# A gate chain on 32 rows, retention tiles normalised in pairs, and three kinds of stores issued one step later

## The chip, the cores and the metric

The kernel runs on one core of a Trainium2 chip. A core has five engines that work side by side: TensorE (PE, with PEld for its weight loads), VectorE (DVE), ScalarE (ACT), GpSimd (POOL) and SyncE (SP). In this kernel SP does almost nothing but issue DMA transfers, in the order in which the program put them into its queue. The engines wait for each other by semaphores, and each carries out its own instructions strictly in order. An instruction that waits therefore also holds up whatever stands behind it on its engine.

The metric is the time of one execution on the device in microseconds (us). Before the change it is 2268.21 us, the median of three runs.

## The reference

The input is one sequence of 1024 rows by 1024 columns. Two layers of the same form follow each other. Each has eight heads of width 256: four mLSTM heads, whose gates depend on the data, and four retention heads, whose decay is fixed. Cut to what matters here:

```python
for l in range(2):
    shift, scale, gate = split(silu(c) @ w_ada[l] + b_ada[l], 3)
    h = rmsnorm(x, norm_g[l]) * (1 + scale) + shift
    mq, mk, mv, mo, mz, mi, mf, rq, rk, rv, rz = split_cols(h @ w_in[l])
    # mLSTM: four heads; mi and mf are one number per row and head
    li, lf = mi + b_igate[l], log_sigmoid(mf + b_fgate[l])
    #   b = cumsum(lf); running maximum m of (li - cumsum(lf)); weights exp(... - m)
    cell = mlstm_chunkwise(silu(conv(mq)), silu(conv(mk)), mv, li, lf)
    y_m = sigmoid(mo) * head_layernorm(cell, gn_m[l]) * silu(mz)
    # retention: four heads; o_t = sum over s <= t of gamma^(t-s) (q_t . k_s) v_s
    ret = retention_chunkwise(rotary(rq), rotary(rk), rv)
    y_r = head_layernorm(ret, gn_r[l]) * silu(rz)
    x = x + gate * (concat(y_m, y_r) @ w_out[l])
return rmsnorm(x, final_g)
```

"Gates" in what follows means the two numbers per row and head, `mi` and `mf`. From them come three running quantities over the 1024 rows of each head: the sum of the coarse part and of the fine part of log sigmoid (`bq`, `br`), and a running maximum (`mx`).

## The kernel before

**Products.** All large products are in fp32, made of three fp32r matmuls each (L177, L178, L179: high by high, high by low, low by high part). The projections use a Strassen-Winograd scheme. Two heads or column groups form a "pair", and a pair needs seven products, named a12, a11, S2, S1, S3, a22, S4, each in two parts for the values. One product of one part is a "slot". A slot of the value stage has 24 matmuls of 256 columns. Products that share a PSUM bank add up in it: a11, S2, S3 and a22 of one part all go through bank X (`px`), so the slot a22 can start only when the sum after S3 has been read out by DVE (L824).

**Steps.** After every slot the program calls `tick()`. Small generators do all side work: a generator does a piece, says `yield n`, and gets its next piece n ticks later (`launch`, L149). PE keeps the order in which the program is written. Each other engine gets an order that a planner sets from its own estimate of times, except for instructions inside `late(...)` (and calls on `Later()`, which wraps every call in it), which keep the order of the program.

**The layer.** At the start of a layer stand the gates' own products (`pgs`, in PSUM bank `pa`), then the chain on the gates, then the value stage of heads 4 and 5 (`v45`), further value, gate and query/key jobs, and the attention of one head after another (retention heads 4 to 7, then mLSTM heads 0 to 3). The order of jobs is a string per layer (`plan`).

**The gate chain (L505 to about L600).** The gates of four heads lie in 4 partitions, 1024 rows along the free axis, in two halves of 512. Bias, absolute value, Exp and Ln run on ACT (L516 to L524). Twelve ticks later some 15 DVE instructions of 4x512 follow for each half; since they are made through `V = Later()`, the trace shows them all at one line, L144. The scans of the second half start from the last column of the first. Results are gathered in a tile `T4` (in the trace `cH` and `cL`), and eight PE transposes of 128x128 (L562) turn them so that rows lie on partitions. `mx` also goes to DRAM (`mdr`, L553) and comes back as `ME` (L567).

**Normalisation (L1153 to L1190).** A retention or mLSTM head is worked through in four chunks j of 256 rows, each of two tiles of 128 rows. In the retention heads some chunks have both tiles computed in one step (j in `WHOLE`), others in two. For a tile: copy from PSUM to `n` (ACT, L1144), mean and variance (DVE, L1160, L1161), `va` (DVE, L1174), the power -1/2 (POOL, L1175), `nmu` (DVE, L1178), scale and shift (ACT, L1180). When both tiles are done, `finish` transposes them (DVE, L1188) into the single buffer `zt` and stores that to DRAM (`ndr`, L1193). `n` too is a single buffer.

**Stores.** `store` (L785 to L798) splits finished values in a high part (ACT, L789) and a low part (DVE, L792 or L794), and a tick later puts two DMA issues into SP's queue (`vdr`, L798). `z_gate` and `o_gate` do the same with gates of the output path (`gdr`, L840 and L848). All of these tiles are buffers of `acc`, of which there are 12 (`NACC`), shared by many jobs. A buffer is free again when its store has read it.

## Time and profile before

| | before |
|---|---|
| runs | 2268.85, 2267.9, 2268.21 us |
| median | 2268.21 us |
| profiled execution, own time | 2268.18 us |
| its span, first to last instruction | 2266.5 us |
| time around the span | 1.7 us |
| mean granted TensorE clock | 0.979 |
| DMA traffic | 448.31 MB, 198 GB/s |

The profiled execution lies 0.03 us below the median. PE is the engine with the largest busy share; the rest of its time consists of waits, and of stretches in which the granted clock is below 1.00, so that a matmul takes longer though PE counts as busy. Where one view gives a row such as "PE px L177 <- DVE acc L824: 12.3, 2, 7.4", PE stood still at a matmul of line 177 that writes `px`, until DVE's instruction of line 824 (which writes `acc`) was done: 12.3 us in all, 2 times, 7.4 us the longest. In rows of the timeline the first number is the start in us from the span's start, the second the duration, and in brackets stands the idle time ahead of the instruction and what ended it. An `x4` behind a row means four instructions in a run.

### The profile page before, as it was taken

What the parts mean: (1) busy time and instruction counts of PE and PEld (TensorE: products, weight loads), DVE (VectorE), ACT (ScalarE), POOL (GpSimd) and SP (SyncE); (2) the same over time, 40 slices, a digit from 0 to 9 for tenths busy, and PEclk for the clock granted to TensorE, in tenths of its full rate; (3) what the DMA queues carried; (4) which work ended last, traced back from release to release, by engine and by line L of the source; (5) the groups of instructions that cost most, each with busy time, mean ns of one, the idle gap of its engine ahead of it and who ended that gap; (6) DMA issues with size and microseconds to landing.
All of it is one profiled execution on the core that took longest, in us unless ns stands there. A gap on an engine that the chain in (4) does not pass through costs nothing.

```text
span 2266.5 us, 35156 instructions
## 1 busy us (share of the span) xinstructions
PE 2151.5 (95%) x11483; PEld 1832.0 (81%) x11483; DVE 1817.5 (80%) x3205; ACT 1159.4 (51%) x2163; POOL 964.3 (43%) x842
## 2 busy tenths in 40 slices
PE   7988999999999999999999799999999899999998
PEld 5787789878898878788778678988987888788886
DVE  6899888989979998784738989788797889977653
ACT  7634345444565656553555434543565565655442
POOL 1443244445454454424366235544544453442313
PEclk9999999999999999999999899999999999999999
DMA  8266688787686777686633767776866686686974
GB/s 285 61 176 186 188 230 249 215 235 202 185 247 175 194 203 186 175 270 210 225 107 84 214 185 210 214 198 185 245 166 192 175 238 186 173 216 203 261 245 118
DMA packets 452549, 448.31 MB, mean 198 GB/s; under 512 B 191219, under 2 KB 309755, under 8 KB 452365
## 3 DMA queue, kind: packets, MB, share of 16 engines
q1 hardware_dynamic: 432636, 410.14, 58.9%
q0 software_dynamic: 19584, 35.66, 10.4%
q8 instruction: 90, 1.47, 0.3%
q14 instruction: 95, 0.77, 0.1%
q10 hardware_dynamic: 144, 0.26, 0.0%
HBM read 322.69 MB, written 123.24 MB: 197 GB/s over the span
## 4 chain that ended last, share of the span: by engine, by line
PE 57%; DVE 22%; DMA 10%; issue 5%; POOL 2%; ACT 2%; SPq 1%; DVEq 0%; POOLq 0%; ACTq 0%
PE px L177 8%; PE px L178 8%; PE px L179 8%; PE pz L179 6%; PE pz L178 6%; PE pz L177 6%; PE pa L177 4%; PE pa L179 4%; PE pa L178 4%; DVE acc L881 3%; DVE R L408 2%; PE pa L1123 2%; DVE acc L626 2%; DMA acc<-kfr 1%; PE pa L1032 1%
## 5 line engine op out<-in xcount | busy, mean ns | idle before, releaser
L403 ACT CAST wH<-R 128x512 fp32r<-128x512 f32 x616 | 377.2, 617 | 476.6 <-PE px L178 133.0
L408 POOL TENSOR_TENSOR R<-R,wH 128x512 fp32r<-128x512 f32 x276 | 397.5, 1447 | 479.5 <-ACT wH L403 325.9
L177 PE MATMUL px<-b,wH 128*128 128x512 f32 x912 | 364.8, 400 | 8.2 <-ACT acc L767 7.4
L179 PE MATMUL px<-b,R 128*128 128x512 f32 x912 | 365.7, 401 | 0.0
L178 PE MATMUL px<-b,wH 128*128 128x512 f32 x912 | 364.8, 400 | 0.0
L408 DVE TENSOR_TENSOR R<-R,wH 128x512 fp32r<-128x512 f32 x340 | 257.2, 760 | 90.5 <-ACT wH L403 87.5
L178 PE MATMUL pz<-b,wH 128*128 128x512 f32 x704 | 280.2, 398 | 1.3 <-DVE b L1262 1.3
L179 PE MATMUL pz<-b,R 128*128 128x512 f32 x704 | 281.0, 399 | 0.0
L177 PE MATMUL pz<-b,wH 128*128 128x512 f32 x704 | 279.8, 397 | 0.2 <-ACT acc L767 0.2
L177 PEld LDWEIGHTS px<-b,wH 128*128 128x128 f32 x912 | 174.6, 191 | 48.1 <-ACT acc L767 8.9
L179 PEld LDWEIGHTS px<-b,R 128*128 128x128 f32 x912 | 174.0, 191 | 42.0 <-POOL R L408 0.8
L178 PEld LDWEIGHTS px<-b,wH 128*128 128x128 f32 x912 | 174.4, 191 | 39.3
L177 PE MATMUL px<-wH,b 128*128 128x256 f32 (+1 forms) x576 | 177.7, 309 | 27.4 <-DVE acc L824 12.3
L178 PE MATMUL px<-R,b 128*128 128x256 f32 (+1 forms) x576 | 174.9, 304 | 3.7 <-DVE R L408 3.7
L179 PE MATMUL px<-wH,b 128*128 128x256 f32 (+1 forms) x576 | 175.8, 305 | 0.0
L701 POOL DMA_DIRECT2D R<-in_w_blk_dram x104 | 92.1, 886 | 185.3 <-DMA R<-in_w_blk_dram 90.8
L178 PEld LDWEIGHTS pz<-b,wH 128*128 128x128 f32 x704 | 133.5, 190 | 32.0 <-DVE b L1262 2.2
L179 PEld LDWEIGHTS pz<-b,R 128*128 128x128 f32 x704 | 133.3, 189 | 31.5
L177 PEld LDWEIGHTS pz<-b,wH 128*128 128x128 f32 x704 | 133.8, 190 | 29.4 <-ACT acc L767 0.6
L177 PEld LDWEIGHTS px<-wH,b 128*128 128x128 f32 x576 | 115.5, 201 | 32.2 <-ACT acc L817 10.4
L179 PE MATMUL pz<-wH,b 128*128 128x256 f32 (+1 forms) x448 | 134.0, 299 | 0.4 <-DVE b L1262 0.4
L177 PE MATMUL pz<-wH,b 128*128 128x256 f32 (+1 forms) x448 | 134.0, 299 | 0.0
(357 smaller groups left out, 5346.7 us busy)
## 6 DMA issues: line engine op xcount, KB each, us to landing
R<-in_w_blk_dram SPq DMA_DIRECT2D x276, 256.0 KB
vdr<-acc SPq DMA_DIRECT2D x128, 256.0 KB
ring<-vdr SPq DMA_DIRECT2D x64, 512.0 KB
R<-in_w_out_dram SPq DMA_DIRECT2D x128, 256.0 KB
R<-in_w_blk_dram POOLq DMA_DIRECT2D x104, 256.0 KB, 4.7
R<-in_w_val_dram SPq DMA_DIRECT2D x80, 256.0 KB
gdr<-acc SPq DMA_DIRECT2D x64, 256.0 KB
acc<-in_w_ada_dram SPq DMA_DIRECT2D x64, 256.0 KB
```

Of the source, the lines that this page charges most:

```text
L177: PE.matmul(o, lt[0], rt[0], start=start, stop=False, skip_group_check=more)
L178: PE.matmul(o, lt[0], rt[1], start=False, stop=False, skip_group_check=more)
L179: PE.matmul(o, lt[1], rt[0], start=False, stop=stop, skip_group_check=more)
L403: A.copy(h, r)
L408: eng.tensor_tensor(lo, r, f(h), ALU.subtract)
L626: V.tensor_tensor(t, f(pair[0]), f(pair[1]), ALU.add)
L701: G.dma_start(raw[n], src, accum_op=ALU.add)
L881: V.scalar_tensor_tensor(acc[:, e:], pt[:, o + e - d:o + HALF - d], wcol, acc[:, e:], ALU.mult, ALU.add)
L1032: PE.matmul(pd, piece(kx[j], i, dt, tt * P, P), qd, start=dt == 0 and i == 0, stop=dt == 1 and i == 1)
L1123: PE.matmul(pi[:, 0:W], piece(qs[j], i, dt, tt * P, P), state[part][:, dt, 0:W], start=part + dt + i == 0, stop=ml and part + dt == 2)
```

## The change

It has three parts.

1. **The gate chain on 32 partitions.** The 1024 rows of the four heads are cut in 8 blocks of 128, so that 4 heads x 8 blocks give 32 partitions with 128 columns. To get there, the biased gates go to DRAM (`gtd`, two stores) and come back in the new shape (two loads). Scans then run inside a block. What one block hands to the next is made by small products on PE: a 32x32 triangular matrix times the last column of each scan (new L547, two matmuls of 32x1), a transpose of the 32 block maxima to one row (new L556), and one matmul that takes the scanned row back to a column (new L561). At the end four PE transposes of 128x32 (new L571) stand in for the eight of 128x128. The chain is stretched over more ticks: it yields 3, 3, 2, 3, 3, 3, 2, 2.
2. **Retention tiles normalised in pairs.** `normalise` is launched once for each chunk, after its second tile, with `va`, power and `nmu` on 128x2.
3. **Stores one tick later.** `yield 1` becomes `yield 2` ahead of the stores of values (L798), of gates (L840, L848) and of heads (L1193).

```diff
@@ -206,6 +206,7 @@
+    gtd = [dpool.tile([2, NH, T], F32, name=f"gtd{l}") for l in range(DEPTH)]
...
@@ -505,63 +506,70 @@
         bg = cols[l][1]
         COL = wt("COL", 8 * 16, 1)
         C4 = COL.rearrange("p (t k h) -> p t k h", t=8, k=4)
-        prev = {}
-        on4 = ones.to_broadcast([P, 512])
-        lfs, lis_, es = [], [], []
-        mxs, fbs, lif = wt("q", 1024, 2), wt("q", 1024, 2), wt("kc", 1024, 1)
+        raw = wt("kc", 1024, 1)
         for half in range(2):
-            pg = pgs[half]
...
-            V.tensor_tensor(lf[0:4], lf[0:4], lfq[0:4], ALU.subtract)
-            bq, br = e, wt("zt", 512, 1) if half else wt("n", 512, 1)
-            yield 1
-            V.tensor_tensor_scan(bq[0:4], on4[0:4], lfq[0:4], prev.get("bq", 0.0), ALU.mult, ALU.add)
-            V.tensor_tensor_scan(br[0:4], on4[0:4], lf[0:4], prev.get("br", 0.0), ALU.mult, ALU.add)
...
-            T4s.append(T4)
-            yield 1
+            for r in (0, 32):
+                A.activation(raw[r:r + 4, half * HALF:(half + 1) * HALF], pgs[half][r:r + 4, :], AF.Identity,
+                             bias=bg[r:r + 4, :])
+        for i in range(2):
+            Q.dma_start(gtd[l][i], raw[32 * i:32 * i + 4, :])
+        one, two = (wt("q", 1024, 2) for _ in range(2))
+        e, bq, br, fb, lfq, lir, tmp, small = (one[0:32, i * P:(i + 1) * P] for i in range(8))
+        u, v, mx, s, li, liq = (two[0:32, i * P:(i + 1) * P] for i in range(6))
+        lower, inc, exc, first = (small[:, i * 32:(i + 1) * 32] for i in range(4))
+        carry = two[0:32, 6 * P:6 * P + 4]
+        on = ones[0:32].to_broadcast([32, P])
+        G.memset(lower, 1.0)
+        l3 = lower.rearrange("p (h t) -> p h t", h=4)
+        G.affine_select(l3, l3, [[-8, 4], [0, 8]], ALU.is_ge, 0.0, base=0, channel_multiplier=1)
+        G.affine_select(lower, lower, [[1, 32]], ALU.is_ge, 0.0, base=-1, channel_multiplier=-1)
+        nc.vector.memset(first, 1.0)
+        nc.vector.memset(first.rearrange("p (h t) -> p h t", h=4)[:, :, 0:1], 0.0)
+        nc.vector.memset(exc, 0.0)
         yield 3
-        for half in range(2):
-            T4 = T4s[half]
-            pt = ps_a()
-            for i in range(4):
-                PE.transpose(pt[:, i * P:(i + 1) * P], T4[:, i * P:(i + 1) * P], ident)
-            V.tensor_copy(C4[:, half * 4:(half + 1) * 4],
-                          pt.rearrange("p (t k h) -> p t k h", t=4, k=4)[:, :, :, 0:4])
+        for i, t in enumerate((fb, li)):
+            Q.dma_start(t, gtd[l][i].rearrange("h (b t) -> (h b) t", t=P))
+        yield 3
+        A.activation(e, fb, AF.Abs)
+        A.activation(e, e, AF.Exp, scale=-1.0)
+        A.activation(e, e, AF.Ln, bias=ones[0:32, 0:1])
+        yield 2
+        V.scalar_tensor_tensor(fb, fb, 0.0, e, ALU.min, ALU.subtract)
+        V.tensor_scalar(lfq, fb, MAG_Q, -MAG_Q, ALU.add, ALU.add)
+        V.tensor_tensor(fb, fb, lfq, ALU.subtract)
+        V.tensor_tensor_scan(bq, on, lfq, 0.0, ALU.mult, ALU.add)
+        V.tensor_tensor_scan(br, on, fb, 0.0, ALU.mult, ALU.add)
+        V.tensor_scalar(liq, li, MAG_Q, -MAG_Q, ALU.add, ALU.add)
+        V.tensor_tensor(lir, li, liq, ALU.subtract)
+        yield 3
+        pc = ps_a()
+        for i, b in enumerate((bq, br)):
+            PE.matmul(pc[0:32, i:i + 1], lower, b[:, P - 1:P], start=True, stop=True)
+        V.tensor_copy(carry[:, 0:2], pc[0:32, 0:2])
+        for i, b in enumerate((bq, br)):
+            V.tensor_scalar(b, b, carry[:, i:i + 1], None, ALU.add)
+        V.tensor_tensor(u, liq, bq, ALU.subtract)
+        V.tensor_tensor_scan(mx, on, u, 0.0, ALU.mult, ALU.max)
+        V.tensor_tensor(v, lir, br, ALU.subtract)
+        yield 3
+        pm = ps_a()
+        PE.transpose(pm[0:1, 0:32], mx[:, P - 1:P], ident[0:32, 0:32])
+        V.tensor_tensor_scan(inc[0:1], first[0:1], pm[0:1, 0:32], 0.0, ALU.mult, ALU.max)
+        V.tensor_tensor(exc[0:1, 1:32], inc[0:1, 0:31], first[0:1, 1:32], ALU.mult)
+        yield 3
+        pb = ps_a()
+        PE.matmul(pb[0:32, 0:1], exc[0:1, :], ones[0:1, 0:1], start=True, stop=True)
+        V.tensor_copy(carry[:, 2:3], pb[0:32, 0:1])
+        V.tensor_scalar(mx, mx, carry[:, 2:3], None, ALU.max)
+        V.tensor_tensor(s, bq, mx, ALU.add)
+        V.tensor_tensor(s, s, br, ALU.add)
+        yield 2
+        Q.dma_start(mdr[l].rearrange("h (b t) -> (h b) t", t=P), mx)
...
@@ -792,7 +800,7 @@
                 V.scalar_tensor_tensor(vL, src, -1.0, f(vH), ALU.mult, ALU.subtract)
             else:
                 V.tensor_tensor(vL, src, f(vH), ALU.subtract)
-            yield 1
+            yield 2
             dst = vdr[l][heads[i]][half * 2 + part].rearrange("(i t p) c -> i p t c", i=2, p=P)
...
         if store is not None:
-            yield 1
+            yield 2
             late(Q.dma_start(store, g))
...
         V.scalar_tensor_tensor(g, th, 1.0, g, ALU.add, ALU.mult)
-        yield 1
+        yield 2
         late(Q.dma_start(store, g))
...
-            elif tts[-1] == 1:
-                launch(normalise(j, (0, 1), [nd3[:, tt, 0:HD] for tt in range(2)]), 1)
+                    A.copy(nrm[j][:, tt, :], po[:, 0:HD])
+            if tts[-1] == 1:
+                launch(normalise(j, [nrm[j][:, tt, 0:HD] for tt in range(2)]), 1)
 
         def gather(nd, po):
...
-            n, a, b = len(tts), tts[0], tts[-1] + 1
+        def normalise(j, src):
             st6 = wt("st6", 12, 2)
...
@@ -1168,25 +1171,26 @@
                 V.tensor_tensor(r, r, gt["em3"][:, h, 2 * j:2 * j + 2], ALU.max)
                 V.scalar_tensor_tensor(va, r, EPS, r, ALU.mult, ALU.mult)
                 V.tensor_tensor(va, va, mv3[:, :, 1], ALU.add)
-                G.tensor_tensor(rs, va, mhalf[:, 0:2], ALU.pow)
             else:
-                e = C_EPS + 2 * h + place(2 * j + a)
-                V.tensor_tensor(va, mv3[:, a:b, 1], kc[:, e:e + n], ALU.add)
-                G.tensor_tensor(rs, va, mhalf[:, 0:n], ALU.pow)
+                e = C_EPS + 2 * h
+                if j in WHOLE:
+                    V.tensor_tensor(va, mv3[:, :, 1], kc[:, e:e + 2], ALU.add)
+                else:
+                    V.tensor_scalar(va, mv3[:, :, 1], kc[:, e:e + 1], None, ALU.add)
+            G.tensor_tensor(rs, va, mhalf[:, 0:2], ALU.pow)
             yield 1
-            nmu = wt("nmu", 2, 2)[:, 0:n]
-            late(V.scalar_tensor_tensor(nmu, mv3[:, a:b, 0], -1.0, rs, ALU.mult, ALU.mult))
-            for i, tt in enumerate(tts):
-                late(A.activation(nrm[j][:, tt, :], src[tt], AF.Identity, scale=rs[:, i:i + 1], bias=nmu[:, i:i + 1]))
-            if tts[-1] == 1:
-                yield 1
-                yield from finish(j)
+            nmu = wt("nmu", 2, 2)
+            late(V.scalar_tensor_tensor(nmu, mv3[:, :, 0], -1.0, rs, ALU.mult, ALU.mult))
+            for tt in range(2):
+                late(A.activation(nrm[j][:, tt, :], src[tt], AF.Identity, scale=rs[:, tt:tt + 1], bias=nmu[:, tt:tt + 1]))
+            yield 1
+            yield from finish(j)
 
         def finish(j):
...
-            yield 1
+            yield 2
```

The instructions of two engines at the places that matter most. First PE in layer 0 (the value stage of heads 6 and 7), before: the eight transposes of the gate chain stand between two slots; `ident` is the identity, `cH` and `cL` are the two T4 tiles, `pz` and `px` banks of value products.

```order
843 L178 MATMUL pz_2214<-R_2098,b_1263 128x256
844 L179 MATMUL pz_2214<-wH_2096,b_1264 128x256
845 L562 MATMUL pa_2241<-ident,cH_1770 128x128 x4
846 L562 MATMUL pa_2247<-ident,cL_1995 128x128 x4
847 L177 MATMUL px_2015<-wH_2173,b_1096 128x256
848 L178 MATMUL px_2015<-R_2175,b_1096 128x256
```

And PE in the changed kernel, layer 0, value stage of heads 4 and 5. The carry matmuls stand between slots S1 and S3 (`q` is the chain's buffer), and the transpose of the maxima between the two parts of a22.

```order
507 L178 MATMUL pz_1636<-R_1497,b_1265 128x256
508 L179 MATMUL pz_1636<-wH_1495,b_1266 128x256
509 L547 MATMUL pa_1663<-q_1228 32x1 x2
510 L177 MATMUL px_1403<-wH_1595,b_1098 128x256
511 L178 MATMUL px_1403<-R_1597,b_1098 128x256
512 L179 MATMUL px_1403<-wH_1595,b_1099 128x256
```

```order
580 L178 MATMUL px_1403<-R_1682,b_1585 128x256
581 L179 MATMUL px_1403<-wH_1680,b_1586 128x256
582 L556 MATMUL pa_1786<-ident,q_1229 1x32
583 L177 MATMUL px_1450<-wH_1676,b_1439 128x256
584 L178 MATMUL px_1450<-R_1678,b_1439 128x256
```

PE's meeting with the gate chain has thus become four short ones, and the first has moved from the stage of heads 6 and 7 ahead of S3 in the stage of heads 4 and 5.

Next DVE in layer 0, before, around the first read-out of bank X after S3 (L824); `R` is a weight tile, `acc` at L144 here is rotary work on 128x256, `q` and `nd` on 4x512 is the gate chain.

```order
179 L144 TENSOR_TENSOR acc_1440<-acc_1440 128x256
180 L824 TENSOR_TENSOR acc_1616<-px_1399,acc_1616 128x512
181 L144 TENSOR_TENSOR acc_1439<-acc_1439,acc_1440 128x256
182 L144 SCALAR_TENSOR_TENSOR q_1220<-q_1220,dm_1222 4x512
183 L144 TENSOR_SCALAR acc_1440<-acc_1441 128x256
184 L144 TENSOR_SCALAR nd_1689<-q_1220 4x512
185 L144 TENSOR_SCALAR acc_1440<-acc_1440 128x256
186 L144 TENSOR_TENSOR q_1220<-q_1220,nd_1689 4x512
```

In the changed kernel (L655 is the former L647, L634 the former L626, L832 the former L824), the first chain instructions of 32x128 stand behind the second pair of L655:

```order
163 L655 SCALAR_TENSOR_TENSOR acc_1527<-acc_1525,acc_1527 128x512
164 L144 SCALAR_TENSOR_TENSOR q_1228<-q_1228 32x128
165 L144 TENSOR_SCALAR q_1228<-q_1228 32x128
166 L144 TENSOR_TENSOR q_1228<-q_1228 32x128
167 L144 SCALAR_TENSOR_TENSOR q_1228<-ones,q_1228 32x128 x2
168 L144 TENSOR_SCALAR q_1229<-q_1229 32x128
169 L144 TENSOR_TENSOR q_1228<-q_1229 32x128
170 L144 CAST acc_1446<-acc_1448 128x256
171 L802 TENSOR_TENSOR acc_1479<-acc_1475,acc_1478 128x512
172 L634 TENSOR_TENSOR acc_1580<-b_1261,b_1262 128x512
```

and around the two read-outs the chain's next ones (COPY of the carries from `pa`, and two additions):

```order
185 L832 TENSOR_TENSOR acc_1628<-px_1403,acc_1628 128x512
186 L144 TENSOR_TENSOR acc_1446<-acc_1446,acc_1447 128x256
187 L144 TENSOR_SCALAR acc_1447<-acc_1446 128x256
188 L144 TENSOR_SCALAR acc_1447<-acc_1447 128x256
189 L144 TENSOR_TENSOR acc_1447<-acc_1447 128x256
190 L144 TENSOR_TENSOR acc_1446<-acc_1446,acc_1447 128x256
191 L144 COPY q_1229<-pa_1663 32x2
192 L832 TENSOR_TENSOR acc_1661<-px_1450,acc_1661 128x512
193 L409 TENSOR_TENSOR R_1757<-R_1307,wH_1755 128x512
194 L144 TENSOR_SCALAR q_1228<-q_1228,q_1229 32x128 x2
195 L800 SCALAR_TENSOR_TENSOR acc_1710<-acc_1628,acc_1709 128x512
196 L409 TENSOR_TENSOR R_1840<-R_1714,wH_1838 128x512
```

The chain's first part has moved from behind the read-out of part 0 to well ahead of it, and the rotary work that stood ahead of that read-out now stands partly behind it.

53 lines of the change are left out of this document (8 added, 45 removed).

## The prediction

> **What bounds the kernel now.** I read four views in this order: the busy shares and the chain that ended last, PE's waits, the timeline around the longest waits, and what DVE did there.
>
> ```profile
> PE 2151.5 (95%) x11483; PEld 1832.0 (81%) x11483; DVE 1817.5 (80%) x3205; ACT 1159.4 (51%) x2163; POOL 964.3 (43%) x842
> ...
> PE 57%; DVE 22%; DMA 10%; issue 5%; POOL 2%; ACT 2%; SPq 1%; DVEq 0%; POOLq 0%; ACTq 0%
> ```
>
> PE is busy for 95% of the span, so work taken off other engines pays only where PE waits for it. DVE holds 22% of the chain that ended last. Which waits these are:
>
> ```profile
> PE px L177 <- DVE acc L824: 12.3, 2, 7.4
> PE pa L1114 <- POOL sL L1071: 10.2, 6, 3.5
> ...
> PE pa L562 <- DVE cL L144: 7.4, 2, 4.4
> PE px L177 <- ACT acc L767: 7.4, 4, 5.4
> ...
> PE pa L345 <- ACT wH L868: 4.0, 1, 4.0
> ```
>
> (Sum, times, longest, in us.) The first, third and last belong to the stage in which the gate chain runs. PE at that stage, layer 0 first and then layer 1:
>
> ```profile
> 120.34 0.28 PE L177 MATMUL px<-wH,b 128*128 128x256 f32 x1
> ...
> 133.66 0.58 PE L177 MATMUL px<-wH,b 128*128 128x256 f32 x1 [7.39 <-DVE acc L824]
> ...
> 179.69 1.12 PE L562 MATMUL pa<-ident,cL 128*128 128x128 f32 x4 [4.39 <-DVE cL L144]
> ```
>
> ```profile
> 1245.76 0.28 PE L177 MATMUL px<-wH,b 128*128 128x256 f32 x1
> ...
> 1256.62 0.55 PE L177 MATMUL px<-wH,b 128*128 128x256 f32 x1 [4.94 <-DVE acc L824]
> ...
> 1297.31 1.11 PE L562 MATMUL pa<-ident,cL 128*128 128x128 f32 x4 [3.00 <-DVE cL L144]
> 1302.42 0.79 PE L345 MATMUL pa<-wH,ones_r 128*128 128x512 f32 x1 [4.01 <-ACT wH L868]
> ```
>
> At 120.34 slot S3 begins, and at 133.66 - 7.39 = 126.27 PE was ready for a22: two slots take 5.93 us, so a tick here is about 3 us. The matmul after each wait is slow, 0.58 against 0.28. The windows (PE, PEld, DVE, ACT, POOL busy, granted clock, DMA share, GB/s) say for how long:
>
> ```profile
> 121.00:180.00 59.00, 44.39 (x338) 43.18 (x338) 58.50 (x99) 20.38 (x36) 25.65 (x15) 0.89 0.65 172
> 134.00:140.00 6.00, 6.00 (x31) 6.00 (x30) 6.00 (x12) 2.69 (x5) 1.74 (x2) 0.53 0.50 175
> 1257.00:1263.00 6.00, 6.00 (x31) 6.00 (x31) 5.93 (x10) 2.68 (x5) 0.88 (x1) 0.53 0.87 291
> 1302.40:1307.00 4.60, 3.98 (x8) 2.37 (x9) 4.00 (x5) 3.77 (x8) 3.77 (x3) 0.50 0.24 42
> ```
>
> After a long wait six us pass at a clock of 0.53, which costs another 6.00 x 0.47 = 2.8 us. And DVE is busy 58.50 of 59 us: in this stage it is the bound, with PE standing 59 - 44.39 = 14.6 us. The chain's own share of it, for layer 1, all at L144:
>
> ```profile
> 1250.00:1300.00 50.00, 24.79 (x38) 0.90 0.77 221
> ```
>
> **Part 1, the gate chain.** Prices come from these rows of DVE, layer 0, then layer 1:
>
> ```profile
> 120.60 1.28 DVE L647 SCALAR_TENSOR_TENSOR acc<-acc,acc 128x512 f32<-128x512 f32 x2
> ...
> 122.61 1.78 DVE L626 TENSOR_TENSOR acc<-b,b 128x512 f32<-128x512 f32 x1
> ...
> 125.61 0.68 DVE L626 TENSOR_TENSOR acc<-b,b 128x512 f32<-128x512 f32 x1
> ...
> 129.07 1.40 DVE L144 TENSOR_TENSOR acc<-acc,acc 128x256 f32<-128x256 f32 x1
> ...
> 132.92 0.68 DVE L824 TENSOR_TENSOR acc<-px,acc 128x512 f32<-128x512 f32 x1
> ```
>
> ```profile
> 1249.35 1.28 DVE L647 SCALAR_TENSOR_TENSOR acc<-acc,acc 128x512 f32<-128x512 f32 x2
> ...
> 1254.13 1.75 DVE L408 TENSOR_TENSOR R<-R,wH 128x512 fp32r<-128x512 f32 x1
> ```
>
> ```profile
> 1291.74 1.27 DVE L144 TENSOR_TENSOR_SCAN q<-ones,q,cf 4x512 f32<-4x512 f32 x1
> ...
> 1298.46 0.22 DVE L144 COPY COL<-pa 128x64 f32<-128x64 f32 x1 [0.29 <-PE pa L562]
> 1298.89 0.68 DVE L338 TENSOR_TENSOR acc<-acc,acc 1x512 f32<-1x512 f32 x1 [0.21 <-DVE COL L144]
> ```
>
> No row has 32x128. A scan of 512 columns takes 1.27, a small copy of 64 columns 0.22; 128 columns are nearer to the latter, so I take 0.22 to 0.4 and a mean of 0.25. The chain has 7 instructions ahead of the first PE meeting, 6 (one copy, two additions, u, scan, v) ahead of the second, 2 ahead of the third, 5 behind: 20 x 0.25 = 5 us in place of 24.8 less some 2 us of closing work that stays. So DVE loses about 18 us of work in each layer, 36 us in all. On ACT the 4x512 work becomes 32x128 and fewer Exp/Ln switches; ACT is at 51% and no PE wait above starts at its gate lines, so I count nothing. The four DMAs of the round trip lie ahead of the value stage, when neither PE nor DVE waits for the gates; if they were late, the first meeting would be late by as much.
>
> Layer 0, step by step. (a) First meeting: DVE is done with the second pair of L647 at 121.88, then 7 x 0.25 = 1.75, so 123.6. PE is there at 120.34: a new wait of 3.3 us. (b) The read-out L824 of part 0: four rotary instructions that ran between 129.07 and 132.92 (3.85, less one weight instruction of about 0.68 that stays) move behind it, the seven of the chain move ahead of it: 133.6 - 3.2 + 1.75 = 132.1. PE, 3.3 us late and on a slow clock, needs S3 until about 123.6 + 5.9 + 2 = 131.5. So a22 starts at 132.1 in place of 133.66, a gain of 1.6, with the slow clock as before. (c) Second meeting: about nine us of DVE work stand ahead of the maxima (five rotary instructions, the second L824, two weight instructions of 0.68 to 1.75, two splits, the chain's six), so they are ready near 139; PE ends a22 of part 0 on a slow clock near 137. New wait 2, and 0.5 at the third meeting. (d) The wait at L562, 4.39, goes, with its slow clock (some 2.0), and 1.2 of the eight transposes. (e) Of the rest of the stage's idle time, 14.6 - 7.4 - 4.4 = 2.8, half goes: 1.4, since DVE is no longer full. Sum: 1.6 - 2.5 + 4.4 + 2.0 + 1.2 + 1.4 = 8 us gained. Bounds: 0, if the second and third meeting wait 5 and 3 each and nothing of (e) comes, to 14, if they do not wait.
>
> Layer 1. DVE ends the second pair at 1250.63, and in the new order one L309 (0.7) stands among the chain's seven: 1253.0. PE is there at 1245.76 and waits 7.2, where it now waits 4.94 a little later. From 1253.0, S3 at half clock to 1260.0, when L824 is long done; a22 starts 3.4 us later than the 1256.62 of before, but the slow clock is then behind it (2.8): 0.6 lost. The wait at L562 goes (3.0 and 1.2 of transposes). The wait at L345, 4.0 with 2.3 of half clock behind it, starts at L338, which stands in DVE's queue behind the copies from L562; without them it can run some ten us earlier if its loads have come, and I count three quarters: 4.7. Sum: 8 gained, with bounds of -1 (L338 stays late) and 12.
>
> Later in layer 0 stands one more wait of that kind, the 5.4 of L767, when ACT waits for DVE's rotary backlog. With 18 us less work on DVE ahead, I count 2, between 0 and 8.
>
> **Part 2, normalisation in pairs.**
>
> ```profile
> L1174 DVE TENSOR_TENSOR va<-mv,kc 128x1 f32<-128x1 f32 (+1 forms) x56 | 24.5, 438 | 0.8
> ...
> L1178 DVE SCALAR_TENSOR_TENSOR nmu<-mv,rsd 128x1 f32<-128x1 f32 (+1 forms) x88 | 38.1, 433 | 24.6 <-POOL rsd L1171 13.6 <-POOL rsd L1175 10.7
> ```
>
> ```profile
> L1175 POOL TENSOR_TENSOR rsd<-va,mhalf 128x1 f32<-128x1 f32 (+1 forms) x56 | 43.7, 781 | 53.2 <-DVE va L1174 49.1 <-DMA R<-in_w_blk_dram 1.7 <-PE px L179 1.1
> ```
>
> Of 56 calls of retention 32 stay (4 chunks x 4 heads x 2 layers). 24 fewer: 24 x (0.438 + 0.433) = 21 us on DVE, 24 x 0.781 = 19 us on POOL. Nearly all lies beside PE. Against it, the first tile of a chunk waits for the second, so the chain behind the last tile grows by one tile's statistics and one ACT pass, a bit over 1 us, which matters where the next head waits for the buffer `n`: six borders between retention heads. For it, the 10.2 us at L1114 wait for POOL, which has less in its queue. I take a gain of 2, between a gain of 10 (all of that wait) and a loss of 7 (six borders x 1.2).
>
> **Part 3, stores a step later.**
>
> ```profile
> ACT acc L789 <- DMA vdr<-acc: 5.6, 2, 3.6
> ACT acc L767 <- DMA vdr<-acc: 4.7, 1, 4.7
> ```
>
> It removes nothing. SP reaches a store later and stands less at it, so loads behind it go out sooner; no PE wait above starts at such a load. Each tile is held one tick, 3 us, longer. Where the ring of 12 buffers is already short (3 times in these rows), the wait can grow by up to 3 each: 9 us of ACT, of which PE's slack takes some two thirds: 3 lost, between a gain of 4 and a loss of 10.
>
> **Sum.** -8 - 8 - 2 - 2 + 3 = -17 against the profiled execution's 2268.18 (0.03 below the median), so 2251. The bounds of the five terms, taken as independent, give about 15 to either side: 2236 to 2266 for this case.
>
> [...] After a wait of only 1.78 us these rows show half rate:
>
> ```profile
> 1227.76 0.39 PE L178 MATMUL px<-R,b 128*128 128x256 f32 x1 [1.78 <-DVE R L408]
> ...
> 1228.58 0.41 PE L178 MATMUL px<-R,b 128*128 128x256 f32 x1
> ```
>
> The matmul 0.8 us behind the wait takes 0.41, as those behind the long waits, so I charge a slow clock to every new wait of two us or more. [...]
>
> **Rivals.**
>
> *The chain is held by POOL.* In the first two L626 rows above the same instruction takes 1.78 and 0.68. The long one lay beside this:
>
> ```profile
> 122.49 3.05 POOL L869 TENSOR_TENSOR b<-acc,b 128x512 fp32r<-128x512 f32 x2 [2.97 <-ACT b L868]
> ```
>
> The chain's seven run just there. If each of POOL's instructions holds one of them to its end, the first meeting moves by up to 3 us in each layer, L824 of layer 0 with it, and the second meeting by 1.5: 9 us of the gain go, 2260. For it: the two rows. Against it: the chain is through at 123.6, when only one of the two has run. [...]
>
> *The waits only move* (no change). If the second and third meeting wait 5 and 3 in both layers, L338 stays late, and parts 2 and 3 cancel: 0 in layer 0, +1 in layer 1, so 2269. For it: DVE stays the bound in this stage, with four meetings where there was one. Against it: 18 us less on an engine that is full for 59 us.
>
> *The ring runs dry* (slower). In the value stages each part makes two tiles per tick; held one tick longer, two to four more of the 12 are taken. ACT's L789 then waits for a store, PSUM is read late, and PE waits. 64 value parts; without part 3 the sum is -20, so it decides from (20 + 4.5) / 64 = 0.38 us each. At 0.48, a sixth of a tick, 31 us: 2279. For it: the rows of part 3 show the ring short already. Against it: three waits in 2266 us.
>
> **Chances.** About 0.2% (4.5 us) is what a measurement of this kernel can tell from no change. Forecast 0.46; still more (below 2236, the later stages gaining from DVE's and POOL's free time) 0.07; held by POOL 0.13, nearly all faster; only moved 0.15, of it 0.13 same; ring dry 0.19, of it 0.16 slower and 0.03 same. Faster 0.65, same 0.17, slower 0.18. The range goes from 2236 to 2274: 0.07 lies below, and of the ring case the part beyond 0.40 us each, some 0.12, above.
>
> **What would show it.** In the profile after: PE's wait at the carry matmuls (new L547) near 3 us in layer 0 and 7 in layer 1; L824's old wait below 3; no wait above 1 us at the four transposes (new L571); L345 below 2; DVE busy below 50 of 59 us in the stage. Part 2: 32 retention powers, and no longer wait for `n` at the borders. Part 3: waits of ACT for `vdr` below 20 us in all. I am wrong if those waits exceed that and PE waits in the value stages, if the two later meetings wait more than 5 us, or if a wait of PE for the round trip of the gates appears.

## The result, and the profile after

The changed kernel takes 2233.6 us (median; 2231.5 to 2236.2), the kernel before 2268.1 us. The ratio is 0.9851, 95% interval 0.9835 to 0.9866: some 34 us, or 1.5%, faster. The forecast was 2251 with 2236 to 2274 as its range. The sign was right; the gain is twice the forecast, and the time lies 2.4 us below the range.

The page of the changed kernel, its busy shares and the chain that ended last:

```profile
PE 2133.3 (96%) x11489; PEld 1818.7 (82%) x11489; DVE 1779.0 (80%) x3139; ACT 1144.5 (51%) x2151; POOL 942.2 (42%) x820
...
PE 44%; DVE 27%; DMA 14%; issue 7%; ACT 3%; POOL 2%; SPq 2%; DVEq 0%; POOLq 0%; ACTq 0%
```

The span fell from 2266.5 to 2229.8 us, by 36.7. PE's busy time fell by 18.2 (2151.5 to 2133.3) although its matmuls are nearly the same: most of that is time at half clock, of which the span has 41 us, before 96. The rest, 18.5, is time in which PE stood still. The mean granted clock of the two profiled executions rose from 0.979 to 0.991, but that is in part chance: the other three executions of the changed kernel had 0.985, 0.987 and 0.987, and 56 others of the kernel before 0.975 to 0.986, with a mean of 0.981. So only about half of the rise can be put down to the change, and of the 18.2 us only a part.

PE's waits, the first seven of that view and one from further down:

```profile
PE pa L547 <- DVE q L144: 10.7, 2, 8.1
PE px L1551 <- DMA b<-in_w_ada_dram: 8.5, 1, 8.5
PE pa L177 <- DVE cf L1099: 7.8, 4, 2.4
PE px L178 <- DVE R L409: 7.8, 3, 5.4
PE px L177 <- ACT acc L775: 5.8, 4, 2.7
PE px L177 <- ACT acc L825: 5.8, 3, 3.1
PE pa L1121 <- POOL sL L1079: 5.8, 5, 2.6
...
PE px L177 <- DVE acc L832: 1.4, 2, 1.1
```

Of the old heads of the list L562 (7.4) is gone, and so is L345 (4.0); L824 (12.3), now L832, is down to 1.4. The wait of the heads for POOL (L1114 before, L1121 now) fell from 10.2 to 5.8. New is the first meeting of PE with the gate chain, L547. PE in the gate stage, layer 0 and then layer 1:

```profile
129.18 0.53 PE L547 MATMUL pa<-q 32*32 32x1 f32 x4 [2.62 <-DVE q L144]
...
137.38 0.39 PE L177 MATMUL px<-wH,b 128*128 128x256 f32 x1 [0.25 <-DVE acc L832]
...
143.49 0.19 PE L556 MATMUL pa<-ident,q 32*1 32x32 f32 x1 [2.96 <-DVE q L144]
```

```profile
1229.56 0.58 PE L547 MATMUL pa<-q 32*32 32x1 f32 x4 [8.07 <-DVE q L144]
```

There is no wait at all at L561 and L571. The stage itself, in the window that was shown of before:

```profile
121.00:180.00 59.00, 53.08 (x414) 51.99 (x413) 53.64 (x125) 22.07 (x40) 20.61 (x16) 0.94 0.70 195
```

PE is busy for 53.1 us of 59 where it was 44.4, with a clock of 0.94 in place of 0.89. DVE has five us of air where it had half a microsecond.

Where along the program the 36.7 us come from can be read off by setting the same matmuls of the two traces side by side. The column is the lead of the changed kernel over the one before (worked out from the starts of PE's rows outside L177 to L179):

| place | lead, us | gained since the row above |
|---|---|---|
| end of layer 0's gate stage (260 us of before) | 8.0 | 8.0 |
| first attention heads (420) | 9.9 | 1.9 |
| end of layer 0's heads (954) | 23.9 | 14.0 |
| start of layer 1's gate stage (1169) | 23.9 | 0.0 |
| end of layer 1's gate stage (1367) | 33.1 | 9.2 |
| layer 1's heads (1573) | 38.6 | 5.5 |
| last row of that kind (2084) | 35.3 | -3.3 |

The two gate stages gave 17.2 us, about what was forecast for them. What the forecast lacks is the 14 us inside the heads of layer 0.

### The profile page after: what moved, and what is told of

The parts are those of the page before. It is cut to its first block, busy times and chain, and to the rows that moved or that the text cites. A ratio compares the mean times of both kernels' runs of the same rounds, so it can differ in the third digit from the quotient of the medians.

```text
span 2229.8 us, 35055 instructions
## 1 busy us (share of the span) xinstructions
PE 2133.3 (96%) x11489; PEld 1818.7 (82%) x11489; DVE 1779.0 (80%) x3139; ACT 1144.5 (51%) x2151; POOL 942.2 (42%) x820
## 4 chain that ended last, share of the span: by engine, by line
PE 44%; DVE 27%; DMA 14%; issue 7%; ACT 3%; POOL 2%; SPq 2%; DVEq 0%; POOLq 0%; ACTq 0%
PE px L177 5%; PE px L178 5%; PE px L179 5%; PE pz L178 4%; PE pz L179 4%; PE pz L177 4%; PE pa L177 3%; PE pa L179 3%; PE pa L178 3%; DVE acc L889 3%; DVE R L409 3%; DMA acc<-kfr 2%; DMA R<-in_w_blk_dram 2%; DVE R L713 2%; DMA R<-in_w_val_dram 2%
## 5 line engine op out<-in xcount | busy, mean ns | idle before, releaser
L409 POOL TENSOR_TENSOR R<-R,wH 128x512 fp32r<-128x512 f32 x276 | 391.4, 1425 | 483.5 <-ACT wH L404 317.0
L177 PE MATMUL px<-b,wH 128*128 128x512 f32 x912 | 360.7, 395 | 6.4 <-ACT acc L775 5.8
L179 PE MATMUL px<-b,R 128*128 128x512 f32 x912 | 362.1, 397 | 0.0
L178 PE MATMUL px<-b,wH 128*128 128x512 f32 x912 | 360.8, 396 | 0.0
L409 DVE TENSOR_TENSOR R<-R,wH 128x512 fp32r<-128x512 f32 x340 | 261.9, 774 | 97.7 <-ACT wH L404 87.7
L179 PE MATMUL pz<-b,R 128*128 128x512 f32 x704 | 280.0, 398 | 0.0
L177 PE MATMUL pz<-b,wH 128*128 128x512 f32 x704 | 279.2, 397 | 0.0
L177 PEld LDWEIGHTS px<-b,wH 128*128 128x128 f32 x912 | 172.2, 189 | 45.4 <-ACT acc L775 7.6
L179 PEld LDWEIGHTS px<-b,R 128*128 128x128 f32 x912 | 171.6, 188 | 40.3
L178 PEld LDWEIGHTS px<-b,wH 128*128 128x128 f32 x912 | 171.9, 188 | 38.6
L177 PE MATMUL px<-wH,b 128*128 128x256 f32 (+1 forms) x576 | 176.9, 307 | 15.9 <-ACT acc L825 5.8
L179 PE MATMUL px<-wH,b 128*128 128x256 f32 (+1 forms) x576 | 174.4, 303 | 0.0
L179 PEld LDWEIGHTS pz<-b,R 128*128 128x128 f32 x704 | 132.8, 189 | 31.3
L177 PEld LDWEIGHTS pz<-b,wH 128*128 128x128 f32 x704 | 133.2, 189 | 28.5 <-issue 0.2
L877 POOL TENSOR_TENSOR kc<-acc,kc 128x512 fp32r<-128x512 f32 x64 | 88.0, 1375 | 114.2 <-ACT kc L876 109.0
L177 PE MATMUL pz<-wH,b 128*128 128x256 f32 (+1 forms) x448 | 134.1, 299 | 0.3 <-DVE acc L785 0.3
L179 PE MATMUL pz<-wH,b 128*128 128x256 f32 (+1 forms) x448 | 133.8, 299 | 0.0
```

The costliest lines, as they stand in the source:

```text
L177: PE.matmul(o, lt[0], rt[0], start=start, stop=False, skip_group_check=more)
L178: PE.matmul(o, lt[0], rt[1], start=False, stop=False, skip_group_check=more)
L179: PE.matmul(o, lt[1], rt[0], start=False, stop=stop, skip_group_check=more)
L409: eng.tensor_tensor(lo, r, f(h), ALU.subtract)
L877: eng.tensor_tensor(dst[1], src, f(dst[0]), ALU.subtract)
```

## The experiments

### The parts, one by one

Each of these kernels is the kernel before with some hunks of the change. The gate chain alone (hunks at L505 to L571 of the new file):

```diff
-        for half in range(2):
-            pg = pgs[half]
...
+            for r in (0, 32):
+                A.activation(raw[r:r + 4, half * HALF:(half + 1) * HALF], pgs[half][r:r + 4, :], AF.Identity,
...
```

with `normalise`, `store`, `z_gate`, `o_gate` and `finish` as they were.

> The gate chain alone; tiles are normalised one by one and stores go out as before. Aligned on the same matmuls, the two traces differ by 8 us at the end of layer 0's gate stage and by 7 to 9 more over layer 1's, so theory 1 (the parts add up, each where it acts) expects 2268 - 17 = 2251 us, waits of PE at the carry matmuls as in the full change, and the waits at L1114 and the slow clock in the heads as before. Theory 2 (the 36 us of DVE work taken away also speed up the attention later) expects 2240 or less. Theory 3 (the planner's new order matters more than the parts) allows anything, with a new wait where the order differs.

Measured: 2249.3 us, ratio 0.9923 (0.9903 to 0.9943): 19 us faster. Aligned on PE's rows, it leads by 8.7 us at the end of layer 0's gate stage and gains 7.1 over layer 1's; the rest comes in the heads, 5.7 us of it in those of layer 0. The sum is that of theory 1, and near the forecast's -18 for the gate chain with its follow-up; the gain in the heads was in neither.

The normalisation in pairs alone (the hunks at `values` and `normalise`, with `finish` as before):

```diff
-                launch(normalise(j, tts, src), 1)
...
+            if tts[-1] == 1:
+                launch(normalise(j, [nrm[j][:, tt, 0:HD] for tt in range(2)]), 1)
```

> Normalisation in pairs alone. Between the gate stages layer 0 gained 16 us and layer 1 some 3. Theory 1, with the gain due to fewer small instructions on DVE and POOL: 2268 - 16 = 2252, and the waits at L1114 nearly gone. Rival, with the gain due to the stores: 2264 to 2270, the waits at L1114 stay. As predicted (a gain of 2): 2266.

Measured: 2259.1 us, ratio 0.9957 (0.9938 to 0.9976): 9 us. The waits at L1114 for POOL are hardly less (9.4 us in 7 waits, before 10.2 in 6), so none of the three expectations fits. That is more than forecast, but what follows shows that it does not add up. By the two traces PE stands still as long as before (115.2 us of the span, before 115.0); what fell is its busy time, 2144.2 us after 2151.5. How the pairs would do that is not shown. DVE's work fell by 9.6 us and POOL's by 16.9, where the forecast had 21 and 19.

The later stores alone:

```diff
-            yield 1
+            yield 2
             dst = vdr[l][heads[i]][half * 2 + part].rearrange("(i t p) c -> i p t c", i=2, p=P)
```

and the same for `gdr` (twice) and `ndr`.

> The stores of values, gates and heads one step later, nothing else. As predicted (3 lost): 2271, and more time of ACT and DVE waiting for vdr. Rival (SP stands less at stores, so loads go out sooner): 2252, with the waits for kfr and qdr loads shorter. Theory 1 says no change: 2266 to 2270.

Measured: 2261.4 us, ratio 0.9975 (0.9960 to 0.9991): 6 us faster, not 3 slower, though less than the rival had it. The ring did not run dry: 6.6 us of ACT's L789 waiting for `vdr`, before 5.6, and L767 no longer waits for it. But ACT's waits for loads are not shorter, as the rival had it: 74.6 us for `kfr` and 47.8 for `qdr`, before 72.3 and 45.5.

Gate chain and pairs, stores as before:

> The change without the later stores. Theory 1 (pairs give the gain in the heads): 2233 to 2236, as the full change or 3 us better. Rival (stores give it): 2250.

Measured: 2248.8 us, ratio 0.9916 (0.9890 to 0.9941). On top of the gate chain (2249.3) the pairs give nothing that can be told. And gate chain with stores, without the pairs:

> The change without the normalisation in pairs. Alone the gate chain gave 19 us, the pairs 9, the stores 7; gate and pairs together 19, all three 34.5. If the stores give what is missing and the pairs nothing: 2234. If the pairs are needed beside the stores (shorter DVE and POOL queues and earlier loads together): 2242 to 2246.

Measured: 2236.7 us, ratio 0.9865 (0.9838 to 0.9892), some 3 us above the full change, with intervals that overlap. So the picture is: gate chain 19, stores 6 alone but 13 to 15 on top of the gate chain, pairs 9 alone but 0 to 3 in company. The forecast had 18, -3 and 2. The stores are what it missed.

### Which stores

On top of gate chain and pairs, one kind of store a step later at a time, one line each (L803 for values, L847 and L855 for gates, L1193 for heads).

> Gate chain and pairs, with only the stores of values (vdr) a step later. Theory 1 (SP stood at stores, and the loads behind them came late): the heads gain from the stores that stand ahead of loads for heads, and vdr is put out mostly before the heads, so 2245 to 2249. Theory 2 (the 15 us come from the values' stage): 2236.

Measured: 2248.2 us (0.9913; 0.9889 to 0.9938). Nothing.

> Gate chain and pairs, with only the stores of output gates (gdr) a step later. In the trace of gate and pairs PE waits 3.56 us at 923.95 for POOL, which waited for a load (dm from mdr) that SP put out only after a store of gdr; in the full change that store stands behind the load. Theory 1: that wait goes, and 2241 to 2245 in all. Theory 2 (chance of the order): no rule, the wait may stay.

Measured: 2244.4 us (0.9901; 0.9871 to 0.9932). About 4 us, at the edge of what can be told. The wait of 3.56 us that the expectation names is down to 0.32 in this trace, so theory 1 holds at that place; in layer 1 a wait at the same line grew from 2.48 to 4.41.

> Gate chain and pairs, with only the stores of heads (ndr) a step later. SP stands at them longest of all, 145 us. Theory 1: loads of keys and queries behind them go out sooner, 2239 to 2243. Theory 2 (the time at ndr is spare): 2248.

Measured: 2237.7 us (0.9869; 0.9846 to 0.9892). 11 us: the stores of heads carry most of it.

What that looks like in one place is seen in gate and pairs, near the end of layer 0, first SP, then POOL, then PE:

```profile
911.15 1.82 SPq L1197 DMA_DIRECT2D ndr<-zt  x4
913.02 0.47 SPq L999 DMA_DIRECT2D acc<-qdr  x1
913.61 0.38 SPq L856 DMA_DIRECT2D gdr<-acc  x1
915.00 0.33 SPq L1021 DMA_DIRECT2D dm<-mdr  x1
```

```profile
920.23 1.49 POOL L1029 TENSOR_SCALAR_AFFINE_SELECT dm<-dm 128x128 f32<-128x128 f32 x2 [2.14 <-DMA dm<-mdr]
921.69 1.25 POOL L409 TENSOR_TENSOR R<-R,wH 128x512 fp32r<-128x512 f32 x1
922.91 0.98 POOL L1079 TENSOR_TENSOR sL<-acc,sH 128x384 fp32r<-128x384 f32 x1
```

```profile
923.95 1.01 PE L1121 MATMUL pa<-ring,sL 128*128 128x258 f32 x3 [3.56 <-POOL sL L1079]
```

SP put out the load of `dm` at 915.00, behind the stores of a head and of a gate. POOL waited for it until 920.23, and with it the weight work and the score tile that stood behind it on POOL, for which PE waited 3.56 us. In the full change the load goes out at 899.55, ahead of the gate's store, and PE arrives at 907.78 with no wait there.

The gain of the later stores has a place. Set beside gate and pairs as in the table above, the full change is 0.5 us behind at the start of layer 0's heads (290), leads by 17.6 at their end (968) and by 18.0 at the end. Nearly all of it comes in the heads of layer 0, although the stores of layer 1 go out later as well.

### Are late loads the cause?

If loads behind stores are what costs, putting the loads out earlier should do as well as putting the stores out later. The table of the attention has an entry for each load of a chunk's keys and queries (`k1`, `q1` and so on); these were moved one step up, on top of gate and pairs:

```diff
-    TABLE = ("q0 k0 d0 t0", "", "v0", "Q0 K0 m0 d1", "s0 k1", "S0", "m1 q1 K1", "v1", "Q1", "V001 t1", "S1 k2 q2", "U01",
-             "s1 d2 K2", "v2 Q2", "V10 U2 m2", "S2", "t2 d3", "V11 U3 k3", "s2 q3", "v3 K3", "Q3 m3", "V20 U4",
+    TABLE = ("q0 k0 d0 t0", "", "v0", "Q0 K0 m0 d1 k1", "s0", "S0 q1", "m1 K1", "v1", "Q1", "V001 t1 k2 q2", "S1", "U01",
+             "s1 d2 K2", "v2 Q2", "V10 U2 m2", "S2", "t2 d3 k3", "V11 U3 q3", "s2", "v3 K3", "Q3 m3", "V20 U4",
```

> Gate chain and pairs, all stores as before the change, but the loads of keys and queries of chunks 1 to 3 of each head are put out one step earlier in the attention's table. Theory (the stores of heads cost because loads of keys and queries stand behind them in SP's queue): most of the 11 us that later stores of heads gave, so 2237 to 2242. Rival 1 (the gain comes from the planner's other order on DVE or from the tile zt, not from the loads): no gain, 2246 to 2252. Rival 2 (the load has to wait for a free acc tile, which the store's step gave): slower than 2249.

Measured: 2256.3 us (0.9945; 0.9929 to 0.9961), 7.6 us slower than gate and pairs. The loads did go out earlier: their issue stands 18.4 us ahead of the scores of the same chunk for `q1` where it was 15.1, and 23.8 where it was 20.1 for `k1` (medians over the 16 heads, worked out from SP's rows and PE's). The theory in that simple form has fallen. The same on the full change:

> The full change, with the same loads one step earlier. Theory: the loads have little left to give, since they now stand ahead of the stores; 2228 to 2234. If a load is still late at every chunk: 2222 to 2227. If the 12 acc tiles are the limit: 2236 or more.

Measured: 2241.8 us (0.9887; 0.9854 to 0.9921), 8 us slower as well. And one step later in place of earlier:

> The full change, with the same loads put out one step later. Theory: what the stores of heads gave is lost, 11 us or more, 2244 to 2255. Rivals 1 and 2: 2231 to 2236, no change.

Measured: 2256.5 us (0.9949; 0.9926 to 0.9973), 23 us slower. Late loads do cost; early ones cost too. Both times with early loads lie where the expectations had put a shortage of `acc` tiles; that was not tried by itself, and SP, which would have to wait for the tile, stands 33.6 us ahead of these loads where it stood 31.3 in gate and pairs.

Nor do the later stores put the loads out earlier on the whole. In the median the load of `q1` stands 15.1 us ahead in gate and pairs, 15.4 with the stores of heads later and 14.8 in the full change. SP stands at the stores of heads for 140.5 us in the full change, after 144.7, and ACT waits 130.1 us for loads of keys and queries, after 128.3. What the later stores change is where single loads stand, and no run here shows which of these places make up the 13 to 15 us.

One step more for the stores of heads:

```diff
         def finish(j):
...
-            yield 2
+            yield 3
```

> The full change, with the stores of heads two steps later than before in place of one. Theory: the swap with the loads is made by the first step, so no more to gain, 2231 to 2236; the tile zt is held longer and the next transpose may wait: up to 2240. If the gain grows with the delay: 2225 or less.

Measured: 2241.4 us (0.9882; 0.9847 to 0.9916): the second step costs 8, a little beyond the 2240 that the expectation gave for the longer hold of `zt`. The gain does not grow with the delay, and SP's time at these stores is not its measure: SP stands there for 92.0 us now, after 140.5, and the kernel is slower.

### SP's queue or the order of the other engines

A store that the program puts out later also changes the planner's estimates, and with them the order in which DVE, ACT and POOL get their work. The two can be separated, since the instructions of these engines are the same in both programs and only stand in another order. In the next four kernels a table holds DVE, ACT and POOL to the order of another kernel by edges between neighbours, which make no engine wait for another. In their traces DVE, ACT and POOL have exactly the order that they were given, and PE's is the same in all; of SP's 1967 issues 1947 to 1954 stand in the order of the kernel with the same stores:

```diff
+    for engine, text in ORDERS.items():
...
+        for a, b in zip(order, order[1:]):
+            tc.add_manual_dep(mine[b], mine[a].name, near, reason="keep_order")
```

Stores at the old step, order of the full change:

> Gate chain and pairs with all stores at their old step, but the order of instructions on DVE, ACT and POOL is held, row by row, to that of the full change. SP's queue stays as in gate and pairs. If the order on the computing engines is what the later stores changed: 2231 to 2239. If SP's queue is: 2245 to 2252.

Measured: 2243.2 us (0.9884; 0.9849 to 0.9919).

> The reverse: the full change with its later stores, SP's queue as in it, and DVE, ACT and POOL held to the order of gate and pairs. If the order on the computing engines decides: 2245 to 2252. If SP's queue does: 2231 to 2239.

Measured: 2247.6 us (0.9894; 0.9866 to 0.9922).

> Gate chain and pairs, all stores at the old step, with DVE, ACT and POOL held to the order of the kernel in which only the stores of heads are later (2237.7). Order decides: 2235 to 2241. SP's queue decides: 2245 to 2252.

Measured: 2244.4 us (0.9891; 0.9851 to 0.9930).

> The reverse of that: stores of heads later, order as in gate and pairs. Order decides: 2245 to 2252. SP's queue decides: 2235 to 2241. Both needed: slower than 2249 here and in the run before.

Measured: 2246.8 us (0.9896; 0.9865 to 0.9926).

| | order of gate and pairs | order of the kernel with later stores |
|---|---|---|
| all stores at the old step | 2248.8 | 2243.2 |
| all stores later | 2247.6 | 2233.6 |
| stores of heads at the old step | 2248.8 | 2244.4 |
| stores of heads later | 2246.8 | 2237.7 |

Two of the four times (2247.6 and 2246.8) lie in the range for "order decides", but their counterparts (2243.2 and 2244.4) lie between the two ranges, and "both needed" had asked for more than 2249. Taken as they stand, SP's queue alone is worth 1 to 2 us, the order alone 4 to 6, and both together 11 to 15. The single effects lie within the intervals, of some 3 to 9 us to either side; that both together give more stands out, since the slowest run with both took 2238.4 us and the fastest of the four tied kernels 2239.4. Whether each needs the other is not shown: no kernel was run that is tied to its own order, and if the table itself cost some 2 to 4 us, the two effects would simply add up.

What SP's part is can be seen where everything but SP stands in the same order. Stores at the old step, order of the full change (SP, ACT, PE; lines one higher than in the full change):

```profile
481.70 1.84 SPq L1198 DMA_DIRECT2D ndr<-zt  x4
483.59 0.45 SPq L1000 DMA_DIRECT2D acc<-qdr  x1
```

```profile
486.33 0.62 ACT L877 CAST q<-acc 128x512 fp32r<-128x512 f32 x1 [2.51 <-DMA acc<-qdr]
```

```profile
489.67 0.98 PE L1122 MATMUL pa<-ring,sH 128*128 128x256 f32 x6 [1.82 <-ACT sH L1079]
```

and the full change at the same instructions:

```profile
472.26 0.38 SPq L999 DMA_DIRECT2D acc<-qdr  x1
472.74 1.97 SPq L1197 DMA_DIRECT2D ndr<-zt  x4
```

```profile
476.05 0.62 ACT L876 CAST q<-acc 128x512 fp32r<-128x512 f32 x1 [1.36 <-DMA acc<-qdr]
```

```profile
480.09 0.98 PE L1121 MATMUL pa<-ring,sH 128*128 128x256 f32 x6 [0.22 <-ACT sH L1078]
```

The four stores take 1.8 to 2.0 us of SP's time to put out. In the one kernel the load of the next queries stands behind them, in the other ahead. ACT waits 2.51 against 1.36 us for the load, and holds back what stands behind it on ACT; PE waits 1.82 against 0.22 at the scores. The 1.2 us between ACT's two waits is not all of PE's 1.6; where the rest comes from was not followed.

### The first meeting with the gate chain

> The full change with PE's first meeting with the gate chain (the carry matmuls) one tick later in layer 0 and three in layer 1, where PE waits 2.6 and 8.1 us for them. If that wait is a cost of its own: 2233.6 - 2.6 - 8.1 - 2.8 of slow clock = 2220. If DVE's read-out of bank X is next in line, as the order on DVE has it (it is done some 3 us before a22 of the full change starts in layer 1, and at the same time in layer 0): the wait moves there and 3 us are gained, 2230. If the planner's other order costs more than that: 2234 or more.

The edit on the full change, and for the second kernel 5 and 3 in place of 6 and 4:

```diff
-        yield 3
+        yield 6 if l else 4
         pc = ps_a()
```

Measured: 2233.4 us (0.9854; 0.9815 to 0.9893), the same as the full change.

> The same in layer 1 alone and two ticks later. If the wait is a cost of its own, 5.8 us of the 8.1 go and some slow clock: 2225. If the read-out is next in line: 2230 to 2232. If order costs more: 2234 or more.

Measured: 2232.5 us (0.9851; 0.9816 to 0.9886), the same too. In the first of the two, layer 1 shows where the 8.07 us went:

```profile
1234.70 0.55 PE L177 MATMUL px<-wH,b 128*128 128x256 f32 x1 [7.17 <-DVE acc L832]
```

It is the read-out of bank X, as before the change. That the wait at L547 is a cost of its own (2220 and 2225) is refuted: in layer 1 it stands in for that read-out. Between the other two expectations, 2230 and 2234, the runs cannot tell. No version here is clearly faster than the full change.

## Why the prediction was half right

**Gate chain: right in size, and only in part in path.** Forecast: 8 us in layer 0, 8 in layer 1, 2 for L767 later. Measured: 19 for the part alone, 8.7 by the end of layer 0's gate stage (which holds L767) and 7.1 in layer 1's. The new waits came out as forecast: at the first meeting 2.6 and 8.1 us (forecast 3.3 and 7.2), at the second in layer 0 3.0 (forecast 2), at L571 and L345 none. DVE's 36 us less are there too (1817.5 to 1781.2 for the part alone). The path to the 8 us of layer 0 was another one, though: a22 of part 0 starts at 137.38, 3.7 us later than before (133.66), where the forecast had it 1.6 earlier, and the waits that went behind it made up for that. So the agreement of the sum there is partly luck. The forecast "DVE busy below 50 of 59 us" was wrong: 53.6, because PE gets through more of the stage in the same window and DVE with it (125 instructions of DVE, before 99). The price of a 32x128 instruction, 0.25 us, was near for most: apart from the scans (0.39 to 0.41) they took 0.19 to 0.28 us, but the five that began while a TENSOR_TENSOR of POOL ran took 1.18 to 1.37 (three of them below).

**Chain held by POOL: the long instructions were there, the price was not.** DVE and POOL in layer 0 of the changed kernel:

```profile
124.92 1.37 DVE L144 SCALAR_TENSOR_TENSOR q<-q 32x128 f32<-32x128 f32 x1
126.33 1.18 DVE L144 TENSOR_SCALAR q<-q 32x128 f32<-32x128 f32 x1
127.54 1.25 DVE L144 TENSOR_TENSOR q<-q 32x128 f32<-32x128 f32 x1
128.72 0.72 DVE L144 TENSOR_TENSOR_SCAN q<-ones,q 32x128 f32<-32x128 f32 x2
129.37 0.19 DVE L144 TENSOR_SCALAR q<-q 32x128 f32<-32x128 f32 x1
129.60 0.28 DVE L144 TENSOR_TENSOR q<-q 32x128 f32<-32x128 f32 x1
```

```profile
124.42 3.01 POOL L877 TENSOR_TENSOR b<-acc,b 128x512 fp32r<-128x512 f32 x2
127.39 1.25 POOL L409 TENSOR_TENSOR R<-R,wH 128x512 fp32r<-128x512 f32 x1
```

Three instructions took 1.2 to 1.4 us each here, where the same operations on 32x128 took 0.27 at 1225.63, 0.19 at 129.37 and 0.27 at 1228.90, with none of POOL's beside them. That is about as long as one POOL instruction (1.25 and, for the two in one row, 1.5 in the mean); the second and third end 0.1 us behind one of POOL's (127.43 and 128.64). So these rows are as the rival had them, though what made the three long was not tried by itself. But PE was only 2.6 us ahead of the chain in spite of it, since PE itself had come later, by this (layer 0, changed kernel, then PE):

```profile
102.48 4.65 DVE L409 TENSOR_TENSOR R<-R,wH 128x512 fp32r<-128x512 f32 x1
```

```profile
107.18 0.58 PE L178 MATMUL px<-R,b 128*128 128x256 f32 x1 [5.40 <-DVE R L409]
```

Before, PE's wait at this place was 1.48 us. The same wait of 5.4 us stands in the traces of the gate chain alone and of gate and pairs. It is 4 us that the forecast did not see; they are already taken off in the 8.0 of layer 0.

**Pairs: 2 forecast, 0 to 3 in company.** Alone they gave 9, on top of the gate chain nothing, with gate chain and stores perhaps 3. Why they act differently alone and in company is not explained by any run here. The work that they take from DVE and POOL was forecast as 40 us and measured 26.5, and it does not show up as such. The 32 powers of retention that were to stay are there.

**Stores: the step that failed.** The term was "3 lost, between a gain of 4 and a loss of 10", from the sentences "It removes nothing" and "no PE wait above starts at such a load". Measured: 13 to 15 us gained in company, 6 alone. With 13 to 15 gained in place of 3 lost the forecast's sum would have come to 2233 to 2235. The second sentence was not so in the trace before. The longest wait of the row L1114, 3.5 us, has such a load behind it (SP, then POOL, then PE):

```profile
916.93 1.83 SPq L1193 DMA_DIRECT2D ndr<-zt  x4
...
919.40 0.39 SPq L848 DMA_DIRECT2D gdr<-acc  x1
920.80 0.33 SPq L1013 DMA_DIRECT2D dm<-mdr  x1
```

```profile
926.82 1.01 POOL L1021 TENSOR_SCALAR_AFFINE_SELECT dm<-dm 128x128 f32<-128x128 f32 x2 [2.61 <-DMA dm<-mdr]
```

```profile
930.07 0.64 PE L1114 MATMUL pa<-ring,sL 128*128 128x258 f32 x3 [3.49 <-POOL sL L1071]
```

The load of `dm` goes out behind a store of a head and a store of a gate, POOL waits 2.61 us for it with the score tile behind, and PE 3.49 us for that tile. The view of PE's waits names only the last link. The forecast put such waits down to the length of POOL's queue. The other half, the order that the planner gives DVE, ACT and POOL once the stores stand elsewhere, was in no term at all, and is worth 4 to 6 us by itself as measured, more together with the queue. How the 13 to 15 us are made up of such places stays open. The waits that the rival "ring runs dry" rested on went rather than grew: there is no wait of ACT for `vdr` among those that the view of the changed kernel shows, 14.5 us before.

**The range.** It was too narrow on the fast side because the stores' bounds were drawn from one mechanism, the ring, which allowed 4 us of gain at most. That a slow clock inside the heads was not charged is not the reason: from gate and pairs to the full change PE stands still 14.5 us less (111.0 to 96.5) and is busy only 3.5 us less (2136.8 to 2133.3).

**Only moved, and more than forecast.** L824 did move in large part: its 12.3 us stand against 10.7 at L547, 3.0 at L556 and 1.4 at L832. L562 (7.4) and L345 (4.0) went without a successor, and the gate chain alone is 19 us faster, so "no change" is refuted. The case "still more, below 2236", which had 0.07, is what happened, though through the stores and not through DVE's and POOL's free time.

**The clock.** In the trace before, a matmul 0.8 us behind a wait of 1.78 us took 0.41 us, against 0.28 at full clock, and in the changed kernel the window behind the wait of 2.62 us at L547 (first row below) has a clock of 0.72. But the forecast's own rule, a slow clock behind every wait of two us or more, does not hold. Behind the first 100 us the changed kernel has ten waits of PE between 2.0 and 3.1 us; six are followed by a stretch at half clock, four are not, such as the 2.71 us at L177 that ended at 224.43 (second row).

```profile
129.00:135.00 6.00, 5.72 (x36) 5.62 (x37) 5.93 (x15) 1.59 (x3) 1.29 (x1) 0.72 0.19 66
...
224.50:229.50 5.00, 5.00 (x22) 4.04 (x23) 4.46 (x6) 3.00 (x6) 2.15 (x2) 1.00 0.83 271
```

What stays open: which places in SP's queue and in the order on DVE, ACT and POOL make up the gain of the later stores, and why it comes in layer 0 alone; why the loads one step earlier cost 8 us; and why the pairs give 9 us alone.

## What to carry to other kernels

When a row of waits names an engine, follow that engine's own wait one or two links further back before saying what does not stand behind it: here a load behind two stores in SP's queue (put out at 920.80, the stores at 916.93 and 919.40) stood behind PE's longest wait for POOL, 3.49 us. When a kernel's engines are ordered by a planner, a move of one DMA is two changes, the queue's and the planner's order; hold one of them to know which one paid, and run a kernel tied to its own order beside it. And see where a removed wait goes: the 8.07 us at L547 came back as 7.17 at a read-out, the 7.4 at L562 went without a successor. Whether clock goes with it differed from wait to wait here: half clock stood behind six of ten between 2.0 and 3.1 us.

## What was not expected of the hardware

One DVE instruction took longer than three POOL instructions beside it. The 128x512 subtraction of L409 at 102.48 took 4.65 us, where the 340 of that line and form took 0.68 us in the median, and the one at 1234.29, with none of POOL's beside it, 0.67. The three stand in one row:

```profile
102.57 4.00 POOL L877 TENSOR_TENSOR b<-acc,b 128x512 fp32r<-128x512 f32 x3
```

It ended at 107.13, half a microsecond behind the last of the three. The trace before has a second such place: of the 48 instructions of L921 that write `b` from `acc` and `kc`, which take 0.48 us in the median, the longest (at 298.85) took 4.61 us, also beside three of POOL. What made the two so long is not shown: that it was the three of POOL is read from their standing side by side, and was not tried by itself.
